# A convolution's running sum moved from SBUF to a PSUM bank, and small sums moved from that bank to another group

## The chip, the cores and the metric

One core of a Trainium2 chip runs the whole program in one launch. The metric is the device time of one execution in microseconds, the median of three runs. The engines are TensorE (PE, with PEld for its weight loads), VectorE (DVE), ScalarE (ACT), GpSimd (POOL) and SyncE (SP, which issues the DMAs).

## The reference

Two blocks on 512 tokens of width 1024, all in float32. The first is an attention block; the change doesn't touch it. The second has a mixer, a cross attention to 256 memory rows, and a feed-forward part. This is the mixer, cut to what matters:

```python
def hybrid_mixer(h, positions, ...):
    proj = h @ w_in
    q, k = partial_rope(proj's q), partial_rope(proj's k)      # 4 heads, 2 x 64 each
    a = diff_attention(q, k, v, lam)                           # softmax(..)[0] - lam * softmax(..)[1]
    a = rmsnorm(a, subln_g) * (1.0 - lam_init)
    c = u[..., :512] * jax.nn.sigmoid(u[..., 512:])            # gated unit
    c = causal_dwconv(c, cv_dw_w) + cv_dw_b                    # 31 taps, 512 channels
    c = jax.nn.silu(layernorm(c, cv_ln_g, cv_ln_b))
    return concatenate([a, c], axis=-1) @ w_out

def cross_attention(h, m, w_cq, w_ckv, w_co):
    q, kv = h @ w_cq, m @ w_ckv                                # kv: the memory projection
    ...
```

## The kernel before

Products of float32 are made of three products of split operands (`mm3` and its like: high by high, high by low, low by high, all at line 131 of the profile); a split is a cast on ScalarE (L149, L224) and a subtraction (L150 for weights on GpSimd or VectorE, L225 on VectorE).

The mixer works on 128 channels by 512 tokens at a time. Its steps are written in a string, in program order:

```python
u0 u1 u2 u3 q0 f0 q1 f1 v1 v0 f3 m b0 b1 b3 c w3 k7 f2 k0 k3 k4 k1 w2 w0 l k5 b2 k2 k6 w1
```

`u` is a quarter of the gated unit (L739 and L740 evacuate its two projections from a linear bank), `q` projects and rotates q and k of two heads (L795 to L800), `v` projects the values (L820), `f` is a head's front: scores, maxima (L843), softmax and difference (L847, L848), with L862 as its last instruction. `b` is a head's back (`diff_back`): transposes, product with the values, column sums of squares (L863 takes them), a root in small steps and a broadcast over partitions. `m` prepares the memory's rows and broadcasts their factors, `k` and `w` are pieces of the memory projection (256 columns; `k` is evacuated at L904), `c` is the convolution and `l` the layer norm over its four results (mean at L965 and L966, then L969, sums of squares, root, broadcast, and L983 to the splits).

The convolution has four quarters `cps[0..3]` of 128 channels. In each, tap 0 is L939, six taps are products on ScalarE (L944, L947) summed by GpSimd (L948) in a tile of their own, and the remaining taps, 92 in all, are one VectorE instruction each (L951): product with a weight per partition plus the running sum. L952 adds GpSimd's part.

PSUM has eight banks, in four groups: three linear ones (`lin`), three for scores (`z`), one `pv`, one small (`sm`). A tile takes the next bank of its group in program order, and waits until the tile that had it is read. Each engine's own order of instructions is made by a scheduler from the program order and these dependencies, with a cost estimate of its own, so that instructions of several steps stand mixed on an engine; on the chip each engine keeps its order.

Of the kernel before, what the change touches and what calls it, by code (L numbers as in the profile page):

```python
# [98 lines left out]
def block_kernel(ctx, tc, wts, vec, c_row, lam_v, cst, x_t, mem_t, mem_n, pos, out):  # L99
# [161 lines left out]
    msb = const.tile([P, P], BF16, name="msb")  # L261
    mfox = const.tile([P, P], BF16, name="mfox")

    def col_sums(accs):

        o = ps_sm()
        for a, acc in enumerate(accs):
            for i in range(NT):
                pe.matmul(o[:, a * NT + i:a * NT + i + 1], lhsT=acc[:, i * P:(i + 1) * P],
                          rhs=ones[:, 0:1], start=True, stop=True)  # L270
        return o[:, :len(accs) * NT]
# [40 lines left out]
            mm(o, ch[:, i:i + 1].to_broadcast([P, P]), identr, i == 0, False)  # L312
            mm(o, cl[:, i:i + 1].to_broadcast([P, P]), identr, False, i == nt - 1)

    def bcast(col, o, nt=NT, eng=dve):

        b = ps_sm()
        bcast_mm(col, b, nt, eng)
        act.copy(out=o, in_=b[:, :nt * P])

# [531 lines left out]
    def diff_back(h, pt, s0):  # L852
        tt = transposed(pt, b2p, {"z": ps_z, "lin": ps_lin, "pv": ps_pv}[TR_TAG])
        pv = ps_pv()
        for c in (3, 2, 1, 0):
            hc = slice(h * P, (h + 1) * P)
            mm3(pv[:, :(c + 1) * P], v2h[:, c, hc], v2l[:, c, hc], tt[c][0], tt[c][1], c == 3, c == 0)
        ah = b2p.tile([P, T], F32, tag="at", bufs=2, name="ah")
        aq = smp.tile([P, T], F32, tag="sq", name="aq")
        act.copy(out=ah, in_=pv)  # L860
        act.activation(out=aq, in_=pv, func=AF.Square)
        dve.scalar_tensor_tensor(out=s0, in0=s0, scalar=EPS, in1=s0, op0=ALU.mult, op1=ALU.mult)  # L862
        dve.scalar_tensor_tensor(out=s0, in0=col_sums([aq]), scalar=1.0 / P, in1=s0, op0=ALU.mult, op1=ALU.add)  # L863
        rsq_bits(s0, s0)
        ar = smp.tile([P, T], F32, tag="sq", name="ar")
        bcast(s0, ar)
        dve.tensor_tensor(out=ah, in0=ah, in1=ar, op=ALU.mult)
        return scaled_split(ah, sg8)

# [6 lines left out]
    def memory():  # L876
        mem_r = mem_t.rearrange("(k p) m -> p k m", p=P)
        msum = b2p.tile([P, 2], F32, name="msum")
        for i in range(2):
            raw = wrp.tile([P, D], F32, tag="wr", name="wr")  # L880
            nc.sync.dma_start(out=raw, in_=mem_n[i * P:(i + 1) * P])
            act.activation(out=raw, in_=raw, func=AF.Square, accum_out=msum[:, i:i + 1])
        rsq(mrc, msum, D)
        for j in range(2):
            raw = wrp.tile([P, D], F32, tag="wr", name="wr")
            nc.sync.dma_start(out=raw.rearrange("p (k m) -> p k m", k=4), in_=mem_r[:, 4 * j:4 * j + 4])
            for a in range(2):
                hi, lo = htile(), htile()
                src = raw[:, a * T:(a + 1) * T]
                for e in range(2):  # L890
                    k = 4 * j + 2 * a + e
                    m = slice(e * NM, (e + 1) * NM)
                    g = V("g_mem", k)
                    act.activation(out=hi[:, m], in_=src[:, m], func=AF.Identity, scale=g)
                    dve.scalar_tensor_tensor(out=lo[:, m], in0=src[:, m], scalar=g, in1=f32(hi[:, m]),
                                             op0=ALU.mult, op1=ALU.subtract)
                    ms.append((hi[:, m], lo[:, m]))
        bcast(mrc, mrb, 2)

    def mem_k(c):  # L900
        o = ps_lin()
# [28 lines left out]
    def conv():  # L930
        for c in range(4):
            cp = cps[c]

            def tap(j):
                return cp[:, 30 - j:30 - j + T], V("cv_w", c * 31 + j)

            ca = b2p.tile([P, PADW], F32, tag="cp", bufs=CP_BUFS, name="ca")[:, :T]
            x_, w_ = tap(0)
            dve.tensor_scalar(out=ca, in0=x_, scalar1=w_, scalar2=V("cv_b", c), op0=ALU.mult, op1=ALU.add)  # L939
            cb_ = (rb[:, 1], nacc[:, 0])[c % 2]  # L940
            for j in range(1, 1 + CONV_POOL):
                x_, w_ = tap(j)
                if j == 1:
                    act.activation(out=cb_, in_=x_, func=AF.Copy, scale=w_)  # L944
                else:
                    pr = b2p.tile([P, T], F32, tag="cpr", bufs=2, name="cpr")
                    act.activation(out=pr, in_=x_, func=AF.Copy, scale=w_)  # L947
                    pool.tensor_tensor(out=cb_, in0=cb_, in1=pr, op=ALU.add)  # L948
            for j in range(1 + CONV_POOL, 31):
                x_, w_ = tap(j)  # L950
                dve.scalar_tensor_tensor(out=ca, in0=x_, scalar=w_, in1=ca, op0=ALU.mult, op1=ALU.add)  # L951
            dve.tensor_tensor(out=ca, in0=ca, in1=cb_, op=ALU.add)  # L952
            cacc.append(ca)
            if c == 1:
                csum.append(nacc[:, 1])
                pool.tensor_tensor(out=csum[0], in0=cacc[0], in1=ca, op=ALU.add)
            elif c == 2:
                pool.tensor_tensor(out=csum[0], in0=csum[0], in1=ca, op=ALU.add)
# [356 lines left out]
```

## Time and profile before

| | us |
|---|---|
| median of three runs (1295.78 to 1298.67) | 1297.72 |
| the profiled execution | 1297.69 |
| its span | 1295.9 |
| TensorE busy | 1203.8 |
| VectorE busy | 849.7 |

The span is the time from the profile's first to its last instruction; 1.79 us of the profiled execution lie around it. The mean granted clock of TensorE was 0.968 of full speed. Busy times are summed over the span; the mixer's part around the convolution is about 507 to 753 us of it.

### The profile page before, as it was taken

The page shows a single profiled execution, that of the slowest core. Times are in us where ns is not written, and L with a number is a line of the kernel's source. Part 1 is how long each engine was busy: PE and PEld are TensorE (multiplying, and loading weights), DVE is VectorE, ACT ScalarE, POOL GpSimd, SP SyncE. Part 2 cuts the span into 40 slices and gives each one's busy share as a digit, 9 for nine tenths or more (in the row PEclk, how much of TensorE's full clock was granted, in tenths as well). Part 3 has the DMA queues.
Part 4 walks back from the last instruction along what each step waited for, and adds up shares of the span by engine and source line. Part 5 has one row for each costly group of instructions (what it writes and reads, how often), then busy time and mean ns, then how long its engine had stood idle before and what let it go on. Part 6 is the DMA issues. An engine that isn't in the chain of part 4 may idle for free.

```text
span 1295.9 us, 16574 instructions
## 1 busy us (share of the span) xinstructions
PE 1203.8 (93%) x6254; PEld 1022.9 (79%) x6254; DVE 849.7 (66%) x1250; ACT 594.5 (46%) x987; POOL 473.5 (37%) x299
## 2 busy tenths in 40 slices
PE   3899999999999999758699999999999999999996
PEld 2788879888878888657688887887888888888886
DVE  6867785655733757999998557456587777771112
ACT  4465655566333553324565635444444444442221
POOL 4534443222122384656543238104422222222222
PEclk9999999999989999879899799999999999999998
DMA  9242222222563332111243244311333332322321
GB/s 368 105 145 75 74 87 69 82 74 94 179 238 99 121 99 82 65 49 57 82 148 125 67 126 146 92 39 66 97 98 98 98 98 98 98 90 90 94 85 65
DMA packets 44960, 134.83 MB, mean 104 GB/s; under 512 B 4945, under 2 KB 10577, under 8 KB 44882
## 3 DMA queue, kind: packets, MB, share of 16 engines
q1 hardware_dynamic: 44882, 133.79, 32.3%
q8 instruction: 49, 0.80, 0.2%
q14 instruction: 29, 0.24, 0.1%
HBM read 124.33 MB, written 6.29 MB: 101 GB/s over the span
## 4 chain that ended last, share of the span: by engine, by line
PE 71%; DVE 20%; ACT 3%; issue 2%; DMA 2%; POOL 1%; SPq 0%; DVEq 0%; POOLq 0%; ACTq 0%
PE lin L131 61%; DVE ca L951 7%; PE z L131 5%; PE pv L131 2%; DMA wr<-in_wts 1%; PE z L457 1%; DVE h L232 1%; DVE ar L374 1%; ACT wh L149 1%; POOL wl L150 1%; DVE wl L150 1%; DVE smc L847 1%; DVE nm L843 1%; DVE h L225 1%; DVE xr L723 1%
## 5 line engine op out<-in xcount | busy, mean ns | idle before, releaser
L131 PE MATMUL lin<-h,wh 128*128 128x512 f32 (+1 forms) x2296 | 709.1, 389 | 11.1 <-ACT h L224 5.0
L131 PEld LDWEIGHTS lin<-h,wh 128*128 128x128 f32 x2296 | 426.2, 190 | 95.1 <-ACT h L224 5.4
L131 PE MATMUL lin<-h,wl 128*128 128x512 f32 (+1 forms) x1148 | 443.9, 387 | 2.7 <-POOL wl L150 1.8
L150 POOL TENSOR_TENSOR wl<-wr,wh 128x1024 fp32r<-128x1024 f32 (+1 forms) x110 | 272.5, 2478 | 461.8 <-ACT wh L149 442.8
L149 ACT CAST wh<-wr 128x1024 fp32r<-128x1024 f32 x189 | 196.7, 1043 | 255.2 <-PE lin L131 194.1
L131 PEld LDWEIGHTS lin<-h,wl 128*128 128x128 f32 x1148 | 217.6, 190 | 44.9 <-POOL wl L150 2.2
L150 DVE TENSOR_TENSOR wl<-wr,wh 128x1024 fp32r<-128x1024 f32 (+1 forms) x79 | 103.0, 1304 | 122.3 <-ACT wh L149 121.6
L131 PE MATMUL lin<-wh,h 128*128 128x256 f32 x656 | 136.5, 303 | 11.3 <-DVE cp L739 9.4
L131 PEld LDWEIGHTS lin<-wh,h 128*128 128x128 f32 x656 | 114.0, 209 | 12.5 <-DVE cp L739 9.6
L951 DVE SCALAR_TENSOR_TENSOR ca<-cp,vecs,ca 128x512 f32<-128x512 f32 x92 | 107.4, 1205 | 0.3
L1138 DVE SCALAR_TENSOR_TENSOR cv<-up,vecs,cv 128x512 f32<-128x512 f32 x88 | 94.5, 1074 | 17.9 <-ACT cv L1136 16.4
L131 PE MATMUL lin<-wl,h 128*128 128x256 f32 x328 | 99.0, 302 | 0.0
L131 PE MATMUL lin<-zz,wh 128*128 128x512 f32 (+1 forms) x324 | 92.4, 370 | 0.0
L131 PEld LDWEIGHTS lin<-wl,h 128*128 128x128 f32 x328 | 68.8, 210 | 0.2
L131 PEld LDWEIGHTS lin<-zz,wh 128*128 128x128 f32 x324 | 58.5, 188 | 11.4
L131 PE MATMUL lin<-zz,wl 128*128 128x512 f32 (+1 forms) x162 | 60.0, 370 | 0.0
L327 POOL TENSOR_TENSOR nacc<-nacc,sq 128x512 f32<-128x512 f32 x34 | 52.5, 1554 | 17.1 <-ACT sq L326 16.7
L1133 POOL MEMSET up<- 128x2 f32 x44 | 4.3, 100 | 148.5 <-DVE cv L1138 116.4
L528 POOL TENSOR_TENSOR zs<-zs,y 64x512 f32<-64x512 f32 x16 | 26.5, 1654 | 72.6 <-DVE y L527 70.3
L542 DVE TENSOR_TENSOR_SCAN om<-om 128x511 f32<-128x511 f32 (+3 forms) x32 | 36.7, 1186 | 8.2 <-ACT om L538 8.0
L1145 ACT ACTIVATE cv<-cv 128x512 f32<-128x512 f32 x22 | 13.9, 632 | 59.9 <-DVE cv L1138 59.9
L1134 DVE TENSOR_TENSOR up<-lin,rb 128x512 f32<-128x512 f32 x44 | 30.1, 687 | 16.3 <-PE lin L131 13.7
(364 smaller groups left out, 1662.6 us busy)
## 6 DMA issues: line engine op xcount, KB each, us to landing
wr<-in_wts SPq DMA_DIRECT2D x189, 512.0 KB, 3.6
ar<-in_wts SPq DMA_DIRECT2D x20, 512.0 KB, 10.2
qk<-qk SPq DMA_DIRECT2D x24, 128.0 KB, 2.2
wr<-in_wts SPq DMA_DIRECT2D x8, 384.0 KB, 3.0
xt<-in_x_t SPq DMA_DIRECT2D x4, 512.0 KB, 5.9
ma_d<-gt SPq DMA_DIRECT2D x8, 256.0 KB, 4.1
ma<-ma_d SPq DMA_DIRECT2D x8, 256.0 KB, 3.4
xr<-in_x_t SPq DMA_DIRECT2D x2, 1024.0 KB, 7.0
```

The source lines that it names most:

```text
L131: pe.matmul(o, lhsT=lhsT, rhs=rhs, start=start, stop=stop, skip_group_check=True)
L149: act.copy(out=hi[:, :n], in_=raw[:, :n])
L150: lo_engine().tensor_tensor(out=lo[:, :n], in0=raw[:, :n], in1=f32(hi[:, :n]), op=ALU.subtract)
L225: dve.tensor_tensor(out=lo, in0=src, in1=f32(hi), op=ALU.subtract)
L232: dve.scalar_tensor_tensor(out=lo, in0=src, scalar=g, in1=f32(hi), op0=ALU.mult, op1=ALU.subtract)
L327: pool.tensor_tensor(out=acc, in0=acc, in1=q, op=ALU.add)
L528: pool.tensor_tensor(out=zs[r], in0=zs[r], in1=y[r], op=ALU.mult)
L542: dve.tensor_tensor_scan(out=om[:, o:e], data0=om[:, o:e], data1=om[:, o:e], initial=1.0, op0=ALU.mult, op1=ALU.bypass)
L951: dve.scalar_tensor_tensor(out=ca, in0=x_, scalar=w_, in1=ca, op0=ALU.mult, op1=ALU.add)
L1134: dve.tensor_tensor(out=up[:, :T], in0=o, in1=rb[:, 0], op=ALU.mult)
L1138: dve.scalar_tensor_tensor(out=r, in0=up[:, 2 - j:2 - j + T], scalar=V("ffn_w", c * 3 + j), in1=r, op0=ALU.mult, op1=ALU.add)
L1145: act.activation(out=a, in_=a, func=AF.Silu)
```

## The change

The convolution's running sum `ca`, an SBUF tile, becomes `cz` in the one bank of `sm`. The four quarters so follow each other through one bank. Only the last instruction, which adds GpSimd's part, writes the SBUF tile `ca`, which is now allocated there. So that the bank is free for this, the column sums and the broadcast of a head's back, and the broadcast of the memory's factors, take a bank of `lin` in place of `sm`. Other users of `sm` stay. The number of instructions that work is the same.

```diff
-    def col_sums(accs):
-        o = ps_sm()
+    def col_sums(accs, ps_=None):
+        o = (ps_ or ps_sm)()
...
-    def bcast(col, o, nt=NT, eng=dve):
-        b = ps_sm()
+    def bcast(col, o, nt=NT, eng=dve, ps_=None):
+        b = (ps_ or ps_sm)()
...
-        dve.scalar_tensor_tensor(out=s0, in0=col_sums([aq]), scalar=1.0 / P, in1=s0, op0=ALU.mult, op1=ALU.add)
+        dve.scalar_tensor_tensor(out=s0, in0=col_sums([aq], ps_lin), scalar=1.0 / P, in1=s0, op0=ALU.mult, op1=ALU.add)
         rsq_bits(s0, s0)
         ar = smp.tile([P, T], F32, tag="sq", name="ar")
-        bcast(s0, ar)
+        bcast(s0, ar, ps_=ps_lin)
...
-        bcast(mrc, mrb, 2)
+        bcast(mrc, mrb, 2, ps_=ps_lin)
...
-            ca = b2p.tile([P, PADW], F32, tag="cp", bufs=CP_BUFS, name="ca")[:, :T]
+            cz = ps_sm()
             x_, w_ = tap(0)
-            dve.tensor_scalar(out=ca, in0=x_, scalar1=w_, scalar2=V("cv_b", c), op0=ALU.mult, op1=ALU.add)
+            dve.tensor_scalar(out=cz, in0=x_, scalar1=w_, scalar2=V("cv_b", c), op0=ALU.mult, op1=ALU.add)
...
             for j in range(1 + CONV_POOL, 31):
                 x_, w_ = tap(j)
-                dve.scalar_tensor_tensor(out=ca, in0=x_, scalar=w_, in1=ca, op0=ALU.mult, op1=ALU.add)
-            dve.tensor_tensor(out=ca, in0=ca, in1=cb_, op=ALU.add)
+                dve.scalar_tensor_tensor(out=cz, in0=x_, scalar=w_, in1=cz, op0=ALU.mult, op1=ALU.add)
+            ca = b2p.tile([P, PADW], F32, tag="cp", bufs=CP_BUFS, name="ca")[:, :T]
+            dve.tensor_tensor(out=ca, in0=cz, in1=cb_, op=ALU.add)
```

In the changed file the lines of the convolution are shifted: tap 0 is L940, the taps are L952, the last addition L954.

VectorE's order at the start of the convolution, before (the numbers behind the names are those of the tiles; `cp_4399` and `cp_4468` are the first two quarters' inputs, `ca_6052` and `ca_6097` their sums, `lin` the gated unit's projections):

```order
L951 SCALAR_TENSOR_TENSOR ca_6052<-cp_4399,vecs_78,ca_6052 128x512 x3
L939 TENSOR_SCALAR ca_6097<-cp_4468,vecs_78 128x512
L951 SCALAR_TENSOR_TENSOR ca_6052<-cp_4399,vecs_78,ca_6052 128x512
L739 TENSOR_TENSOR cp_4537<-lin_4539,rb_4291 128x512
L951 SCALAR_TENSOR_TENSOR ca_6097<-cp_4468,vecs_78,ca_6097 128x512
L951 SCALAR_TENSOR_TENSOR ca_6052<-cp_4399,vecs_78,ca_6052 128x512
L951 SCALAR_TENSOR_TENSOR ca_6097<-cp_4468,vecs_78,ca_6097 128x512
L951 SCALAR_TENSOR_TENSOR ca_6052<-cp_4399,vecs_78,ca_6052 128x512
```

And now, from the first addition to the first rotation (L795):

```order
L952 SCALAR_TENSOR_TENSOR sm_6052<-cp_4399,vecs_78,sm_6052 128x512 x4
L739 TENSOR_TENSOR cp_4537<-lin_4539,rb_4291 128x512
L952 SCALAR_TENSOR_TENSOR sm_6052<-cp_4399,vecs_78,sm_6052 128x512 x5
L740 TENSOR_TENSOR sg_4601<-lin_4570,rb_4291 128x512
L952 SCALAR_TENSOR_TENSOR sm_6052<-cp_4399,vecs_78,sm_6052 128x512 x6
L739 TENSOR_TENSOR cp_4606<-lin_4608,rb_4291 128x512
L952 SCALAR_TENSOR_TENSOR sm_6052<-cp_4399,vecs_78,sm_6052 128x512 x6
L740 TENSOR_TENSOR sg_4670<-lin_4639,rb_4291 128x512
L952 SCALAR_TENSOR_TENSOR sm_6052<-cp_4399,vecs_78,sm_6052 128x512 x2
L795 TENSOR_TENSOR ro_4788<-h_4785,cosb_4366 128x64
```

Two quarters went side by side there, and 40 additions stood ahead of the first rotation (4, 7, 7, 7 and 15 between the evacuations); now one quarter goes alone, and 23 stand there. The second quarter begins after the first one's last addition, which takes GpSimd's part `rb_4291`, behind two rotations:

```order
L799 TENSOR_TENSOR h_4798<-ro_4801,ro_4802 128x8x8
L800 TENSOR_TENSOR h_4798<-ro_4803,ro_4804 128x8x8
L954 TENSOR_TENSOR ca_6096<-sm_6052,rb_4291 128x512
L940 TENSOR_SCALAR sm_6098<-cp_4468,vecs_78 128x512
L952 SCALAR_TENSOR_TENSOR sm_6098<-cp_4468,vecs_78,sm_6098 128x512 x3
L795 TENSOR_TENSOR ro_4924<-h_4921,cosb_4366 128x64
```

The last quarter's last addition stood ahead of the first L904; now it stands behind the backs of heads 0 and 1 and within the front of head 2, and all eight L904 stand behind that front.

TensorE's order at the start of the memory projection, before (`lin_5532` is the last product of the values, `lin_6234` the first of the memory projection, step w3):

```order
L131 MATMUL lin_5532<-wh_5589,h_4277 128x256
L131 MATMUL lin_5532<-wl_5590,h_4277 128x256
L131 MATMUL lin_5532<-wh_5589,h_4278 128x256
...
L131 MATMUL lin_6234<-wh_6237,h_5764 128x256
L131 MATMUL lin_6234<-wl_6238,h_5764 128x256
L131 MATMUL lin_6234<-wh_6237,h_5765 128x256
```

And now (the same step is `lin_6238`; `lin_6033` is the broadcast of head 3's back, `lin_6011` its column sums, `pv_6813` and `pv_6822` transposes of head 2's back):

```order
L131 MATMUL z_6420<-kl0o_4394,qk_6340 128x256
L131 LDWEIGHTS identb_90
L131 MATMUL z_6420<-mfox_94,identb_90 128x128
L269 MATMUL lin_6011<-ones_86,aq_6007 128x1 x4
L457 MATMUL pv_6813<-idf_79,p_6363 128x128
...
L457 MATMUL pv_6822<-idf_79,p_6363 128x128
L131 MATMUL lin_6033<-identr_91,bch_6034 128x128
L131 MATMUL lin_6238<-wh_6241,h_5764 128x256
L131 MATMUL lin_6238<-wl_6242,h_5764 128x256
```

The 384 matmuls of the memory projection began four transposes after the last product of the values and stood among the fronts of heads 3 and 2 and the backs of heads 0, 1 and 3. Now they begin behind all of these: 264 of them, the norm's mean and sums, 24, the sums and the broadcast of head 2's back, and the last 96.

## Rows read from the trace of the kernel before

**Rows 1.** The page's first part: busy time, share of the span, instructions.

```profile
PE 1203.8 (93%) x6254; PEld 1022.9 (79%) x6254; DVE 849.7 (66%) x1250; ACT 594.5 (46%) x987; POOL 473.5 (37%) x299
```

**Rows 2.** The chain that ended last: start, duration, engine, tile, line, count.

```profile
538.54 24.65 DVE ca L951 x15
```

**Rows 3.** Stretches of the mixer: busy time of each engine, granted clock, DMA.

```profile
core 0: us, PE busy (x) PEld busy (x) DVE busy (x) ACT busy (x) POOL busy (x), PEclk, DMA share, GB/s
507.00:545.00 38.00, 28.63 (x159) 25.63 (x158) 37.93 (x37) 10.73 (x14) 21.67 (x10) 0.87 0.20 67
545.00:602.00 57.00, 38.84 (x278) 37.11 (x277) 56.62 (x71) 22.41 (x36) 35.19 (x20) 0.85 0.17 51
602.00:665.00 63.00, 49.38 (x337) 46.49 (x338) 62.32 (x107) 36.53 (x79) 33.08 (x18) 0.86 0.31 96
665.00:723.00 58.00, 52.08 (x390) 47.91 (x388) 52.25 (x117) 36.36 (x82) 25.58 (x12) 0.96 0.44 135
723.00:753.00 30.00, 28.60 (x188) 27.65 (x188) 17.98 (x43) 16.38 (x25) 9.15 (x4) 0.79 0.19 54
```

**Rows 4.** The tile ca: count, ns min/median/max, first and last start.

```profile
L951 DVE SCALAR_TENSOR_TENSOR ca<-cp,vecs,ca x92: 727/742/2893, 507.7 to 670.2; 128x512 f32<-128x512 f32 x92
```

**Rows 5.** Timeline of VectorE, 530 to 575: start, duration, instruction.

```profile
533.23 4.71 DVE L951 SCALAR_TENSOR_TENSOR ca<-cp,vecs,ca 128x512 f32<-128x512 f32 x7
...
570.44 2.97 DVE L951 SCALAR_TENSOR_TENSOR ca<-cp,vecs,ca 128x512 f32<-128x512 f32 x4
```

**Rows 6.** Timeline of GpSimd at 539, with the idle time before.

```profile
539.29 1.74 POOL L742 TENSOR_TENSOR cp<-cp,sg 128x512 f32<-128x512 f32 x1 [7.79 <-ACT sg L741]
```

**Rows 7.** Groups of GpSimd, 507 to 672: busy us, mean ns, idle before.

```profile
L150 POOL TENSOR_TENSOR wl<-wr,wh 128x1024 fp32r<-128x1024 f32 x18 | 47.7, 2652 | 27.7 <-ACT wh L149 27.7
L948 POOL TENSOR_TENSOR rb<-rb,cpr 128x512 f32<-128x512 f32 x12 | 18.8, 1571 | 2.8 <-ACT cpr L947 2.6
```

**Rows 8.** Groups of VectorE over the whole span.

```profile
L1134 DVE TENSOR_TENSOR up<-lin,rb 128x512 f32<-128x512 f32 x44 | 30.1, 687 | 16.3 <-PE lin L131 13.7 <-ACT rb L319 2.6
...
L798 DVE TENSOR_TENSOR ro<-h,sinb 128x64 f32<-128x64 f32 x8 | 6.1, 763 | 0.0
...
L904 DVE TENSOR_TENSOR kvo<-lin,mrb 128x256 f32<-128x256 f32 x8 | 3.3, 417 | 0.1
```

**Rows 9.** Timeline of VectorE from 717 on.

```profile
717.81 2.46 DVE L969 SCALAR_TENSOR_TENSOR ca<-lin,ca 128x512 f32<-128x512 f32 x4
...
722.07 0.22 DVE L847 SCALAR_TENSOR_TENSOR smc<-s,nlam,smc 128x1 f32<-128x1 f32 x1 [0.29 <-ACT p L845]
...
722.79 0.15 DVE L862 SCALAR_TENSOR_TENSOR s<-s 128x4 f32<-128x4 f32 x1
...
727.05 0.16 DVE L309 TENSOR_TENSOR bcl<-s,bch 128x4 fp32r<-128x4 f32 x1 [0.26 <-ACT bch L308]
...
736.26 2.48 DVE L983 TENSOR_TENSOR ca<-ca,lin 128x512 f32<-128x512 f32 x4 [2.71 <-PE lin L131]
...
748.50 0.68 DVE L225 TENSOR_TENSOR h<-ca,h 128x512 fp32r<-128x512 f32 x1
```

**Rows 10.** VectorE's line L847 alone in the fronts after 665.

```profile
665.00:723.00 58.00, 8.69 (x11) 0.96 0.44 135
```

**Rows 11.** Timeline of TensorE at the end of the gated unit.

```profile
523.12 0.28 PE L131 MATMUL lin<-wh,h 128*128 128x256 f32 x1
...
533.36 0.58 PE L131 MATMUL lin<-wh,h 128*128 128x256 f32 x1 [9.37 <-DVE cp L739]
```

**Rows 12.** Timeline of TensorE from the last product of the values to the stage's end.

```profile
664.49 0.28 PE L131 MATMUL lin<-wh,h 128*128 128x256 f32 x1
664.61 0.40 PE L131 MATMUL lin<-h,wh 128*128 128x256 f32 x2
...
715.10 1.02 PE L965 MATMUL lin<-nacc,ones 128*128 128x512 f32 x2
...
730.78 0.47 PE L131 MATMUL lin<-identr,bch 128*128 128x128 f32 x1
...
751.91 0.28 PE L131 MATMUL lin<-wh,h 128*128 128x256 f32 x1
```

## The prediction

> **What bounds the kernel now.** I read the page's head first: TensorE is busy for 93% of the span [rows 1]. So a change on VectorE counts only where TensorE waits for it. Next comes the chain that ended last. In the mixer of the second block it runs through the convolution's VectorE instruction; its longest piece is 24.65 us for fifteen of them [rows 2]. The table by stage shows the stage of the change, 507 to 753 us: up to 665 VectorE is busy for 37.93 of 38, 56.62 of 57 and 62.32 of 63 us, and TensorE for 28.63, 38.84 and 49.38 [rows 3]. From 723 it turns round: TensorE 28.60 of 30, VectorE 17.98. So the first 160 us are VectorE's, the last 30 TensorE's, and what lies between is both. Outside the stage nothing changes, so the whole answer is where the mixer's last 256-column matmul stands (751.91 us before).
>
> The convolution's 92 tap additions (L951) take 107.41 us, 727 to 2893 ns each with a median of 742 [rows 4]. The timeline says why they spread: seven follow each other in 4.71 us from 533.23 [rows 5], where GpSimd stands idle for 7.79 us up to 539.29 [rows 6], and the next fifteen are the 24.65 us of the chain, when it works again. In 507 to 672 its part is eighteen weight subtractions (L150) and two times twelve tap sums (L948) [rows 7]. VectorE instructions of the same size that read one operand from PSUM don't spread: forty-four average 687 ns [rows 8].
>
> **What each part of the change does.**
>
> *Taps in PSUM.* Each of the 92 then has one SBUF operand and the running sum in PSUM. Its price: no row shows VectorE writing PSUM at this size. From below, four PSUM-reading ones follow each other in 2.46 us [rows 9], about 0.61 each. From above, the contended mean of today, 107.41/92 = 1.17. Of one chain back to back in SBUF the trace has four in 2.97 us, the first on another tile: (2.97 − 0.73 − 0.66)/2 = 0.79, against (4.71 − 0.74)/6 = 0.66 for the alternating tiles of before [rows 5]. The new order has one chain at a time (one bank), first in runs of four to six and later one by one between other instructions. I take 0.70, nearest to the SBUF chain's rows: 92 × 0.70 = 64 us. Today's 107.4 overlap by some 0.08 each, so they cover 100. The saving is 36 us of VectorE.
>
> The Trainium skill's page "SBUF — State Buffer", section "Who interferes with whom", says that a VectorE instruction with two SBUF inputs contends with a GpSimd instruction that reads SBUF, and one with at most one does not; the trace agrees (727 to 2893 ns against 687). The Trainium skill's page "Perfetto Trace Analysis", section "Optimizing Scalar/DVE Operations", speaks against the change: about 125 ns of access overhead for VectorE on PSUM, about 60 on SBUF. By that the 92 would cost 92 × 0.065 = 6 us more and the end be 1306 (an estimate from that page); the PSUM-reading rows here show no such penalty for reading.
>
> *VectorE up to the end of the fronts.* From 507 to 723 it is busy for 37.93 + 56.62 + 62.32 + 52.25 = 209.1 us and idle for 6.9 [rows 3]. Less the 36. Less the norm's four (2.46) and five evacuations of the memory projection (L904, 0.417 each [rows 8]), which move behind: 4.5. Less contention in the fronts after 665: there the eleven instructions of L847 take 8.69 us [rows 10], where an undisturbed one takes 0.22 [rows 9], so 6.3 are excess, and by the same look at L848, L288 and L309 I put as much again; GpSimd does there the memory weights' subtractions, which now wait for banks (next part). I take 13 off, with 0 and 20 as bounds. Busy: 209.1 − 36 − 4.5 − 13 = 155.6.
>
> Idle comes in at the front. Between the evacuations of the gated unit and the first rotation VectorE's order has 4, 5, 6, 6 and 2 additions, where it had 4, 7, 7, 7 and 15. TensorE's stall of 9.37 us behind L739 [rows 11] mostly goes. But VectorE reaches the rotation at 507 + 23 × 0.79 + 4 × 0.6 = 528, and the first projection, begun at 523.12 [rows 11], needs 96 × 0.12 = 11.5 us plus the copy to SBUF: 7 us of wait. Then L954 of the first channel, which now must come before the second channel can begin (L940 takes the one bank again), waits for GpSimd's six sums: an estimate from their 1.57 us and the subtractions between [rows 7] puts these at 542, 4.5 us more. Behind it stand the other rotations, so TensorE's scores wait too. With the 6.9 of before: 18.5 idle. The last front then ends at 507 + 155.6 + 18.5 = 681, where before has 722.79 [rows 9]: 42 us gained there. TensorE allows it: the six projections of q, k and v are 576 matmuls, 69 us from 523, with scores and transposes about 605.
>
> *Small sums in the linear banks.* This gives the gain back. The three linear banks go round in program order. The sums and broadcasts of the heads' back parts (b0, b1, b3) stand in it before the memory projection, so TensorE's order no longer begins with that when the v projection ends (as at 664.49 to 664.61 [rows 12]) and works on it under f3 and f2. It begins it behind b3's broadcast, which waits for VectorE: the front's end plus the root's small steps (722.79 to 727.05 before, 4.3 us [rows 9]): 681 + 4 = 685. From there everything is serial:
> - 264 matmuls at 0.12 [rows 12]: 31.7 us.
> - The norm: before, from 715.10 (mean) to 730.78 (broadcast) 15.7 us [rows 12], with other work between on every engine. I take 11, part of b2's products within: of the 15.7 the fronts' and b2's instructions fill about a third.
> - 24 matmuls and the rest of the broadcast: 3.
> - From L983 to the last split before: 736.26 to 749.18, 12.9 us [rows 9]. b2's broadcast now stands behind that split on VectorE and ahead of 96 matmuls on TensorE; six matmuls and eight column sums are all its cover. Bounds 8 and 13; I take 10.5.
> - 96 matmuls, the broadcast and the rest of b2's products: 13.4.
> - After two waits TensorE's granted clock falls to half, as in 723 to 753 (0.79 [rows 3]): 1.5.
>
> Sum 71 us; the stage ends at 685 + 71 = 756. b2's broadcast, which came after 752 in before and held TensorE there for 1.7, is then done: 754.3 against 751.9 [rows 12]. The change costs 2.4 us. Against the profiled execution, 1297.69 (the span and 1.79 around it), that is 1300.1; the median shown, 1297.72, is the same to 0.03. I say **1300**.
>
> **Rivals.**
>
> *The gain reaches the end.* If VectorE's other instructions before 665 lose their stretching too (their neighbours on GpSimd run faster without L951), or the waits at the front are hidden, b3's broadcast comes at about 670: 670 + 71 − 1.7 = 739, 1285. For it: the rotation's step L798 averages 763 ns for 64 columns [rows 8], more than 512 columns from PSUM. Against: GpSimd has the same work in less time. Below 680 for that broadcast the change is a gain of over 0.2%.
>
> *A longer tail.* If the single bank leaves VectorE idle for another 10 us (it waits for six GpSimd sums at each channel's end, with nothing of the convolution to fill in), b3's broadcast is at 695, and if the norm's waits are as long as before (15.7 and 12.9) the tail is 78: 695 + 78 − 1.7 = 771, 1317. It decides from b3's broadcast after 685 with a tail of 71 (the sum above stands at that edge), or from a tail over 71 behind 685. For it: the order has nothing beside those waits on TensorE. Against: less GpSimd contention there.
>
> *Adding in one PSUM bank is slow.* If write and next read of the same bank cost 0.95 us, the 92 take 23 us more: 1323. For it: nothing here shows such a chain, and the SBUF chain already goes from 0.66 to 0.79. Against: PSUM reads at 0.61. The overhead that the Trainium skill's page "Perfetto Trace Analysis" states, in the section named above, would be a quarter of this.
>
> *The change doesn't do what it says:* the taps stay as stretched as before, with one SBUF operand too. Then 36 us of VectorE come back while the serial tail stays: 1336. Against it stand the forty-four at 687 ns, though GpSimd is less busy beside those.
>
> **How the numbers follow.** The trade 0.50, the gain at the end 0.27, the longer tail 0.15, slow PSUM 0.05, no relief 0.03. About 0.2% (2.6 us) is what a measurement of this kernel can tell from no change. The likeliest case's own range is 1292 to 1309 (8 us either way on 685, from the 13 off and the front's idle, and 4 on 71). Of it 0.08 lie below 1295, 0.17 within, 0.25 above 1300.3. Faster: 0.08 + 0.27 = 0.35; same: 0.17 and 0.02 from the edge of the longer tail: 0.19; slower 0.46. The range takes in the gain down to 1278 and the longer tail to 1319.
>
> **What the profile after would show.** Right: the taps 0.65 to 0.80 us each, with a narrow spread; TensorE without the 9 us stall at 524 but with the memory projection beginning late, at 677 to 693, behind a broadcast into a linear bank; gaps of TensorE of some 10 us in the norm and again before b2's broadcast; the first 512-column matmuls of the output product near 754. Wrong: taps over 0.9 us, or memory matmuls under the fronts of heads 3 and 2, or b3's broadcast before 675 or after 695.

## The result and the profile after

The changed kernel takes **1304.17 us** (median; 1300.48 to 1306.35) where the kernel before, on the same chips, takes 1296.89. The ratio is 1.0058, with a 95% interval of 1.0044 to 1.0072: the change costs 7.3 us, between 5.7 and 9.3. The forecast of 1300.0 had the sign and the mechanism, and a price of 2.4 us that is too low by about five. The profiled execution took 1302.44 us, its span is 1300.5, and the mean granted clock 0.963.

The page's first part of after, against [rows 1]:

```profile
PE 1209.3 (93%) x6254; PEld 1025.0 (79%) x6254; DVE 802.7 (62%) x1250; ACT 596.3 (46%) x987; POOL 460.2 (35%) x299
```

VectorE's busy time falls by 47 us and the kernel gets slower: less time of this engine is not by itself less time of the kernel. The five stretches of [rows 3], after the change:

```profile
core 0: us, PE busy (x) PEld busy (x) DVE busy (x) ACT busy (x) POOL busy (x), PEclk, DMA share, GB/s
507.00:545.00 38.00, 38.00 (x260) 35.39 (x258) 28.48 (x44) 17.40 (x26) 30.05 (x18) 1.00 0.30 91
545.00:602.00 57.00, 46.95 (x358) 44.18 (x357) 55.94 (x96) 37.99 (x73) 36.72 (x24) 0.93 0.29 91
602.00:665.00 63.00, 44.34 (x234) 36.54 (x233) 62.35 (x145) 29.31 (x72) 9.15 (x5) 0.74 0.16 51
665.00:723.00 58.00, 48.45 (x337) 45.46 (x335) 21.26 (x60) 25.58 (x48) 27.54 (x12) 0.85 0.42 119
723.00:753.00 30.00, 18.95 (x121) 18.70 (x121) 12.63 (x33) 13.44 (x20) 6.01 (x3) 0.72 0.11 39
```

Read the matmul counts. In the first two rows TensorE issues 618 where it issued 437: the stall behind the gated unit is gone. From 602 to 665 it issues 234 instead of 337, at a granted clock of 0.74: it has run out of work and waits on the chains of the fronts and backs. What released it last was ScalarE's softmax (L844) in 7.5 us of these waits, VectorE in 5.7 and a transfer of `qk` in 3.2, and VectorE, which feeds these chains, is as full as before. In the last row, 723 to 753, it is busy for 18.95 of 30 us where it was busy for 28.60. What was won in front is lost behind. The tap additions themselves, in the view of the tile `sm`, against [rows 4]:

```profile
L952 DVE SCALAR_TENSOR_TENSOR sm<-cp,vecs,sm x92: 731/754/757, 506.9 to 667.8; 128x512 f32<-128x512 f32 x92
...
L940 DVE TENSOR_SCALAR sm<-cp,vecs x4: 803/806/814, 505.6 to 637.4; 128x512 f32<-128x512 f32 x4
L954 DVE TENSOR_TENSOR ca<-sm,rb x2: 691/692/692, 540.8 to 635.6; 128x512 f32<-128x512 f32 x2
```

The spread of 727 to 2893 ns has become 731 to 757. VectorE's timeline at the front, and where the fronts end (against [rows 5] and [rows 9]):

```profile
514.93 4.70 DVE L952 SCALAR_TENSOR_TENSOR sm<-cp,vecs,sm 128x512 f32<-128x512 f32 x6
...
525.36 1.54 DVE L952 SCALAR_TENSOR_TENSOR sm<-cp,vecs,sm 128x512 f32<-128x512 f32 x2
533.93 0.52 DVE L795 TENSOR_TENSOR ro<-h,cosb 128x64 f32<-128x64 f32 x1 [7.04 <-ACT h L788]
...
540.78 0.69 DVE L954 TENSOR_TENSOR ca<-sm,rb 128x512 f32<-128x512 f32 x1 [1.32 <-POOL rb L949]
...
675.86 0.15 DVE L862 SCALAR_TENSOR_TENSOR s<-s 128x4 f32<-128x4 f32 x1
...
680.47 0.15 DVE L309 TENSOR_TENSOR bcl<-s,bch 128x4 fp32r<-128x4 f32 x1
```

The first L952 row is one chain back to back: (4.70 − 0.76)/5 = 0.79 us each. The last front ends at 675.86 where it ended at 722.79. And TensorE from there, against [rows 12]:

```profile
679.97 0.47 PE L131 MATMUL lin<-identr,bch 128*128 128x128 f32 x1 [0.77 <-ACT bch L308]
680.24 0.52 PE L131 MATMUL lin<-wh,h 128*128 128x256 f32 x1
...
716.64 1.02 PE L967 MATMUL lin<-nacc,ones 128*128 128x512 f32 x2
...
722.70 1.36 PE L131 MATMUL lin<-ones,cpr 128*128 128x1 f32 x8 [3.55 <-POOL cpr L977]
...
726.18 1.86 PE L131 MATMUL lin<-ones,cpr 128*128 128x1 f32 x8 [2.12 <-POOL cpr L977]
729.77 0.48 PE L131 MATMUL lin<-identr,bch 128*128 128x128 f32 x1 [1.73 <-ACT bch L308]
...
735.28 0.95 PE L269 MATMUL lin<-ones,aq 128*128 128x1 f32 x8
...
743.43 0.48 PE L131 MATMUL lin<-identr,bch 128*128 128x128 f32 x1 [7.20 <-ACT bch L308]
...
757.57 0.63 PE L131 MATMUL lin<-h,wh 128*128 128x512 f32 x2
```

680.24 is the first matmul of the memory projection, right behind the first one of the broadcast of head 3's back, as forecast: before it stood at 664.61, under the fronts. The four bracketed waits from 722.70 on have nothing beside them. The stage ends at 757.5, 5.5 us later than before.

**How stages are compared below.** The first tap (L939, L940) starts between 501.4 and 507.1 us in the profiled executions of the fourteen kernels, though no edit is made to what lies ahead of it. So a stage's length is taken here from the start of its own first tap to the start of the last addition of the output product (into `xr`), in one profile of each kernel: 295.3 us before, 300.9 after. "Broadcast" is that of head 3's back (VectorE's L309 in it), from the first tap: 220.4 us before, 174.9 after. Ratios are of medians, to the kernel before on the same chip (1294.96 to 1295.34 us).

### The profile page after: what moved, and what is told of

It is laid out like the page before. It is cut to its first block, busy times and chain, and to the rows that moved or that the text cites. A ratio compares the mean times of both kernels' runs of the same rounds, so it can differ in the third digit from the quotient of the medians.

```text
span 1300.5 us, 16580 instructions
## 1 busy us (share of the span) xinstructions
PE 1209.3 (93%) x6254; PEld 1025.0 (79%) x6254; DVE 802.7 (62%) x1250; ACT 596.3 (46%) x987; POOL 460.2 (35%) x299
## 5 line engine op out<-in xcount | busy, mean ns | idle before, releaser
L150 POOL TENSOR_TENSOR wl<-wr,wh 128x1024 fp32r<-128x1024 f32 (+1 forms) x110 | 268.0, 2438 | 486.6 <-ACT wh L149 467.6
L150 DVE TENSOR_TENSOR wl<-wr,wh 128x1024 fp32r<-128x1024 f32 (+1 forms) x79 | 103.0, 1304 | 125.3 <-ACT wh L149 124.6
L131 PE MATMUL lin<-wh,h 128*128 128x256 f32 x656 | 126.2, 290 | 2.5 <-DVE v2l L820 2.5
L131 PEld LDWEIGHTS lin<-wh,h 128*128 128x128 f32 x656 | 106.5, 197 | 2.9 <-DVE v2l L820 2.8
L131 PE MATMUL lin<-wl,h 128*128 128x256 f32 x328 | 95.4, 291 | 0.0
L952 DVE SCALAR_TENSOR_TENSOR sm<-cp,vecs,sm 128x512 f32<-128x512 f32 x92 | 69.0, 750 | 1.3
L131 PEld LDWEIGHTS lin<-wl,h 128*128 128x128 f32 x328 | 64.8, 197 | 0.1
L131 PE MATMUL z<-qk 128*128 128x512 f32 (+3 forms) x96 | 37.8, 398 | 11.7 <-ACT p L844 6.4
L542 DVE TENSOR_TENSOR_SCAN om<-om 128x511 f32<-128x511 f32 (+3 forms) x32 | 36.7, 1187 | 8.2 <-ACT om L538 8.0
```

The costliest lines, as they stand in the source:

```text
L131: pe.matmul(o, lhsT=lhsT, rhs=rhs, start=start, stop=stop, skip_group_check=True)
L150: lo_engine().tensor_tensor(out=lo[:, :n], in0=raw[:, :n], in1=f32(hi[:, :n]), op=ALU.subtract)
L542: dve.tensor_tensor_scan(out=om[:, o:e], data0=om[:, o:e], data1=om[:, o:e], initial=1.0, op0=ALU.mult, op1=ALU.bypass)
L952: dve.scalar_tensor_tensor(out=cz, in0=x_, scalar=w_, in1=cz, op0=ALU.mult, op1=ALU.add)
```

## Experiments

The prediction's theory, called A, is the trade: taps in PSUM save about 36 us of VectorE, and the small sums in the linear banks make TensorE's memory projection wait for a broadcast, so that the saving is lost behind it.

### 1. The banks alone

```diff
-            cz = ps_sm()
+            ca = b2p.tile([P, PADW], F32, tag="cp", bufs=CP_BUFS, name="ca")[:, :T]
...
-                dve.scalar_tensor_tensor(out=cz, in0=x_, scalar=w_, in1=cz, op0=ALU.mult, op1=ALU.add)
+                dve.scalar_tensor_tensor(out=ca, in0=x_, scalar=w_, in1=ca, op0=ALU.mult, op1=ALU.add)
```

> Only the small sums move to the linear banks; the taps stay in an SBUF tile. Theory A (the linear banks' order puts the memory projection behind head 3's broadcast, and only the faster taps pay for that): the projection begins behind that broadcast at about 715 to 725 us, since the taps are as stretched as before, and a serial tail of some 78 us follows as in the changed kernel: the stage ends 35 to 50 us later than before, 1330 to 1347. Theory B (the single bank and the single chain of the convolution are what cost the gain, the sums' new place is neutral): 1292 to 1302, as before.

Measured: 1325.87 us, 1.0248 [1.0229, 1.0267]. Half of the change alone costs 31 us by the medians, and the other half gives some 24 back, since the whole costs 7. TensorE, at the broadcast and at the stage's end:

```profile
703.73 0.47 PE L131 MATMUL lin<-identr,bch 128*128 128x128 f32 x1
704.00 0.52 PE L131 MATMUL lin<-wh,h 128*128 128x256 f32 x1
...
782.11 0.63 PE L131 MATMUL lin<-h,wh 128*128 128x512 f32 x2
```

From broadcast to end 78.4 us, in after 77.6: the tail is the same whatever the taps cost. It starts 22.7 us later, counted from the first tap, because VectorE is late: over its stretch from the first tap to the last front it is busy for 188.85 of 194.15 us, in after for 157.53 of 170.45. So the 31.3 us of busy time that the PSUM taps save arrive as 23.7, the rest is VectorE's waits at the front (idle 5.3 to 12.9). The time lies below A's 1330 to 1347 and far above B's 1292 to 1302. A's size was too large because the fronts end at 700.62: taking the memory projection from under them relieves VectorE more than A had it. VectorE's groups up to the last front show where (line, busy us, mean ns, idle before); before:

```profile
L951 DVE SCALAR_TENSOR_TENSOR ca<-cp,vecs,ca 128x512 f32<-128x512 f32 x92 | 107.4, 1205 | 0.3
...
L847 DVE SCALAR_TENSOR_TENSOR smc<-s,nlam,smc 128x1 f32<-128x1 f32 x16 | 10.8, 672 | 2.2 <-ACT p L845 2.0
```

and with the banks alone:

```profile
L951 DVE SCALAR_TENSOR_TENSOR ca<-cp,vecs,ca 128x512 f32<-128x512 f32 x92 | 107.2, 1203 | 0.3
...
L847 DVE SCALAR_TENSOR_TENSOR smc<-s,nlam,smc 128x1 f32<-128x1 f32 x16 | 4.4, 274 | 0.7 <-ACT p L845 0.6
```

The taps keep their price to 0.2 us; L847 falls by 6.4.

### 2. The small sums in the bank `pv`

```diff
-        dve.scalar_tensor_tensor(out=s0, in0=col_sums([aq], ps_lin), ...)
+        dve.scalar_tensor_tensor(out=s0, in0=col_sums([aq], ps_pv), ...)
...
-        bcast(s0, ar, ps_=ps_lin)
+        bcast(s0, ar, ps_=ps_pv)
```

(and the same for the memory's factors)

> The taps in PSUM as in the change, the small sums in the bank of the products with the values (pv) in place of the linear ones. Theory A: the memory projection begins when the values are done (about 607 us) and runs under the fronts, the 264 matmuls (32 us) leave the tail, head 3's broadcast stays at 680 to 690: 1268 to 1282. Theory B: the taps' single bank keeps holding everything up: 1300 to 1306, as the change.

Measured: 1288.63 us, 0.9953 [0.9934, 0.9972], between A's 1268 to 1282 and B's 1300 to 1306; the stage is 287.5 us long, 13.4 less than after. With the linear banks free of broadcasts the memory projection starts under the fronts again. Two stretches:

```profile
600.00:665.00 65.00, 56.21 (x422) 53.48 (x421) 63.19 (x111) 30.41 (x60) 32.27 (x14) 0.93 0.46 141
665.00:720.00 55.00, 37.12 (x148) 30.66 (x149) 32.59 (x96) 24.77 (x58) 4.89 (x3) 0.55 0.07 24
```

422 matmuls up to 665 against 234 of after in nearly the same time. But `pv` is one bank, which the backs' products need too: behind 665 TensorE is busy for 37 of 55 us, at a granted clock of 0.55, and 19.4 us of its waits stand before instructions that write `pv`. Head 3's broadcast, which A had at 680 to 690, comes at 715.9. The wait has moved from one bank group to another. That the bank group decides A's loss is shown here, and that `pv` has a wait of its own.

### 3. Part of the memory projection ahead of the backs

The bank groups stay as the change has them; two orders of steps put 168 and 72 of the memory projection's matmuls ahead of the backs.

```diff
-MIX = "... f3 m b0 b1 b3 c w3 k7 f2 k0 k3 k4 k1 w2 w0 l k5 b2 k2 k6 w1"
+MIX = "... f3 m w3 k7 k0 k3 k4 k1 b0 b1 b3 c f2 w2 w0 l k5 b2 k2 k6 w1"
```

> The change, with six pieces of the memory projection (w3 k7 k0 k3 k4 k1, 168 matmuls) placed ahead of the backs of heads 0, 1 and 3 in the program order; banks as in the change. Theory A: 168 x 0.12 = 20 us leave the tail and hide under the fronts: 1281 to 1291. Theory B: no change, 1300 to 1306.

```diff
+MIX = "... f3 m w3 k7 b0 b1 b3 c f2 k0 k3 k4 k1 w2 w0 l k5 b2 k2 k6 w1"
```

> The same with two pieces only (w3 k7, 72 matmuls). Theory A: 72 x 0.12 = 8.6 us leave the tail: 1292 to 1299. Theory B: 1300 to 1306.

Measured: with 168 ahead 1291.98 us, 0.9978 [0.9959, 0.9997], a microsecond above A's range; with 72 ahead 1301.87, 1.0063 [1.0044, 1.0082], in B's. Against after the stages are 10.9 and 0.2 us shorter, where 168 and 72 matmuls at 0.12 are 20 and 8.6. What is missing stands in the broadcast, 12.2 and 7.6 us later than in after. Matmuls moved under the fronts are no gift: the fronts end later with them. What comes with them are evacuations, weight subtractions and a share of TensorE's order; only the subtractions are tested alone, in experiment 4. Two rows of VectorE with 168 ahead:

```profile
634.00 2.31 DVE L862 SCALAR_TENSOR_TENSOR s<-s 128x4 f32<-128x4 f32 x1
636.24 0.41 DVE L904 TENSOR_TENSOR kvo<-lin,mrb 128x256 f32<-128x256 f32 x1
```

L862, four elements a row, takes 2.31 us there, beside the last of three weight subtractions that end on GpSimd at 636.29, and 0.15 or 0.16 in each of the four fronts of after. An evacuation L904 that stood behind the fronts now stands within them.

### 4. The memory weights without their low part

To see how much of those 12.2 us GpSimd's subtractions (L150) make, these two kernels leave them out for the memory weights: the products with the low part take the high part again, so all matmuls stay. One has the order with 168 ahead, the other, as control, the order of the change.

```diff
-    def unit(name, j, n=D):
+    def unit(name, j, n=D, lo=True):
...
+        if not lo:
...
+            return hi, hi
...
-        lin_k(o[:, :NM], unit("mk", c), 0, ms)
+        lin_k(o[:, :NM], unit("mk", c, lo=False), 0, ms)
...
```

(and the same for the weights of the memory's values)

> As the kernel with 168 matmuls of the memory projection ahead of the backs, but the memory projection's weights have no low part: GpSimd's subtractions (L150) for these twelve weights are left out and the high part stands in for the low one, with the same matmuls. Theory C (moving the projection back under the fronts gave only half of its 20 us, since GpSimd's subtractions then stretch VectorE's instructions in the fronts and head 3's broadcast comes 12 us later): that broadcast falls from 692.6 to 681 to 685, time 1280 to 1285. Theory D (the fronts are slowed by what else the projection brings, its evacuations and its share of TensorE and ScalarE): as without this edit, 1289 to 1295.

> Control: the change itself with the same subtractions left out. They stand in the tail there, where VectorE waits anyway, so by both theories nothing moves: 1299 to 1306.

Measured: 1286.87 us, 0.9934 [0.9916, 0.9953], between C's range and D's, and the control 1297.87, 1.0019 [1.0003, 1.0035], a microsecond below what both theories said. The broadcast stands at 187.1 us from the first tap with 168 ahead, at 179.2 without the subtractions; in after at 174.9, in the control at 171.8. So the price of 168 matmuls under the fronts is 12.2 us with the subtractions and 7.4 without: by these single profiles they make 4.8 of it, under half. L862 is back at 0.16 us. The control moved by 3 us as well, so the subtractions cost something wherever they stand. What makes the other 7.4 (evacuations, TensorE's time itself) was not taken apart.

### 5. The norm and head 2's back in the score banks

The tail's waits come from the norm and from head 2's broadcast, which hold the linear banks in program order. Here they get banks of `z`, whose scores are done by then.

```diff
-        lmean = ps_lin()
+        lmean = ps_z()
...
-        lvar = ps_lin()
+        lvar = ps_z()
...
-        lr = ps_lin()
+        lr = ps_z()
...
+        ps_ = ps_z if h == 2 else ps_lin
```

(`ps_` is then the group of head 2's sums and broadcast.)

> The change, with the layer norm's three tiles and head 2's sums and broadcast in banks of the scores (z), so that they don't stand in the linear banks' order. Theory A2 (the tail's two waits, 13.1 us from the norm's mean to its broadcast and 8.2 before head 2's broadcast, are bare only because the next memory pieces need the banks of these tiles): the 384 matmuls run through both, the stage ends at 735 to 740: 1281 to 1288. Rival (the chain from the norm's mean over its splits to head 2's is itself as long as the tail): 1296 to 1304.

Measured: 1283.99 us, 0.9905 [0.9869, 0.9941], as A2 had it; the stage is 287.4 us, 13.5 less than after. Its stretch from 690 to 730, the norm's mean and the step on VectorE before its broadcast, and head 2's broadcast:

```profile
690.00:730.00 40.00, 40.00 (x334) 39.87 (x333) 11.95 (x22) 23.70 (x34) 28.17 (x12) 1.00 0.60 185
```

```profile
672.42 2.02 PE L968 MATMUL z<-nacc,ones 128*128 128x512 f32 x2
...
702.99 0.17 DVE L309 TENSOR_TENSOR bcl<-muc,bch 128x4 fp32r<-128x4 f32 x1 [0.26 <-ACT bch L308]
...
734.74 1.09 PE L131 MATMUL lin<-h,wh 128*128 128x512 f32 x4
...
740.55 0.33 PE L131 MATMUL z<-identr,bch 128*128 128x128 f32 x1 [1.50 <-ACT bch L308]
```

TensorE is busy for 40.00 of 40 us through the second half of the norm and its broadcast, at full clock, and the output product's 512-column matmuls begin at 734.74, in after at 757.57; head 2's broadcast stands among them, where after waits 7.20 us for it. The norm itself is not faster: from its mean to its broadcast it takes 30.6 us (672.42 to 702.99), in after 13.1. Head 3's broadcast, with the norm's mean now ahead of it, comes 7.0 us later than in after (181.9 us from the first tap). Neither matters, since the norm has lost its hold on the banks and the memory projection runs beside it. So the waits of the tail are a matter of bank groups too, and the trade need not be one.

### 6. Both, and how many taps GpSimd takes

The order with 168 ahead on experiment 5's banks, with `l b2` ahead of the pieces that are left; and on that the number of a quarter's taps that go to ScalarE and GpSimd, nine and five where it was seven (seven products on ScalarE, not six, which GpSimd sums in six additions).

```diff
+MIX = "... f3 m w3 k7 k0 k3 k4 k1 b0 b1 b3 c f2 l b2 w2 w0 k5 k2 k6 w1"
```

> Both cures: 168 matmuls ahead of the backs, the norm and head 2's sums in z banks, and the norm and head 2's back ahead of the last 216 matmuls. By A2, with head 3's broadcast at 692 and 216 matmuls, products and broadcasts behind (26 + 9 us): stage end 727 to 733, 1272 to 1280. By the rival: 1286 to 1293.

```diff
-CONV_POOL = 7
+CONV_POOL = 9
```

> The best so far (z banks and 168 matmuls first, 1281.8) with eight taps of each quarter instead of six summed by GpSimd: VectorE loses 8 x 0.70 = 5.6 us, GpSimd gets 8 x 1.5 = 12. If VectorE's own time sets head 3's broadcast: 5 us earlier, 1276 to 1279. If VectorE waits for GpSimd's sums at a quarter's end (1.32 us today) or is stretched by them elsewhere: 1281 to 1288.

```diff
-CONV_POOL = 7
+CONV_POOL = 5
```

> The other way: four taps of each quarter on GpSimd, VectorE gets 5.6 us more, GpSimd 12 less. If VectorE's own time sets the broadcast: 1285 to 1289. If GpSimd's sums cost VectorE's other instructions more than they save (1.3 us for each that is stretched): 1275 to 1281.

Measured: with seven 1281.78 us, 0.9884 [0.9853, 0.9916]; with nine 1278.91, 0.9878 [0.9839, 0.9916]; with five **1273.56**, 0.9837 [0.9799, 0.9876]. The stages are 280.5, 281.3 and 273.4 us. The kernel with seven misses both of its ranges (1272 to 1280 and 1286 to 1293): head 3's broadcast comes at 695.3 where 692 was taken, and the last 256-column matmul at 736.5 where 727 to 733 was expected. Nine taps off take eight additions from VectorE and win nothing that can be told. Their median lies in the range that was given for a gain from VectorE's own time, but head 3's broadcast is not 5 us earlier: it comes 193.2 us from the first tap, with seven 190.1. Five taps off give VectorE eight additions more and win 7.1 us of the stage, some 6 by the ratios of the medians; that is the side of contention, 1.4 us below the range given for it. With nine, VectorE's timeline has two long waits for projected heads that ScalarE has not yet copied:

```profile
535.50 0.51 DVE L795 TENSOR_TENSOR ro<-h,cosb 128x64 f32<-128x64 f32 x1 [8.51 <-ACT h L788]
...
547.02 0.35 DVE L795 TENSOR_TENSOR ro<-h,cosb 128x64 f32<-128x64 f32 x1 [6.01 <-ACT h L788]
```

With seven they are 7.04 and 0.78. With five, the first wait is 5.46, the second is gone, and the last addition of the first quarter, which with seven waits 1.32 for GpSimd, does so no more:

```profile
529.77 0.51 DVE L795 TENSOR_TENSOR ro<-h,cosb 128x64 f32<-128x64 f32 x1 [5.46 <-ACT h L788]
...
531.59 0.69 DVE L955 TENSOR_TENSOR ca<-sm,rb 128x512 f32<-128x512 f32 x1
```

More than the waits, other instructions got cheaper. VectorE's groups from the first tap to the convolution's last addition, with seven taps off:

```profile
L953 DVE SCALAR_TENSOR_TENSOR sm<-cp,vecs,sm 128x512 f32<-128x512 f32 x92 | 69.1, 751 | 1.3
...
L799 DVE TENSOR_TENSOR h<-ro 128x64 f32<-128x64 f32 x8 | 8.0, 996 | 0.1
...
L798 DVE TENSOR_TENSOR ro<-h,sinb 128x64 f32<-128x64 f32 x8 | 5.0, 630 | 0.0
```

and with five:

```profile
L953 DVE SCALAR_TENSOR_TENSOR sm<-cp,vecs,sm 128x512 f32<-128x512 f32 x100 | 75.0, 750 | 1.7
...
L799 DVE TENSOR_TENSOR h<-ro 128x64 f32<-128x64 f32 x8 | 4.9, 610 | 0.0
...
L798 DVE TENSOR_TENSOR ro<-h,sinb 128x64 f32<-128x64 f32 x8 | 1.7, 213 | 0.0
```

The eight additions cost 5.9 us more. The rotations, whose operands lie in SBUF, cost less: their six lines, L795 to L800, fall from 31.3 us in sum to 18.7. Over the whole stretch VectorE is busy for 148.58 us with seven and 143.34 with five, so all but the taps went from 79.5 to 68.3. The Trainium skill's page "Perfetto Trace Analysis", section "Optimizing Scalar/DVE Operations", warns that offloading between VectorE and GpSimd might not help, because they share an SBUF read port; these two kernels agree, by 7.1 us of the stage.

### 7. Where the memory projection stands

Two more orders on the same banks, seven taps off: the 168 matmuls among the backs, and 240 of the 384 ahead of them.

```diff
+MIX = "... f3 m w3 b0 k7 k0 b1 k3 k4 b3 c k1 f2 l b2 w2 w0 k5 k2 k6 w1"
```

> As the best so far, but the 168 matmuls' pieces stand between the backs of heads 0, 1 and 3 in place of ahead of them. If what counts is only that they come before head 3's broadcast: 1279 to 1284. If their banks then wait for each back's broadcast: later by up to 5 us, 1283 to 1288.

```diff
+MIX = "... f3 m w3 k7 k0 k3 k4 k1 k5 k2 k6 b0 b1 b3 c f2 l b2 w2 w0 w1"
```

> As the best so far with all nine 256-column key pieces ahead (w3 and all k, 240 matmuls in place of 168). By the full price 72 x 0.12 = 8.6 us leave the tail: 1273 to 1276. By what the earlier runs showed (of 8.6 us moved under the fronts 0.2 came back, of 20 us 11) the fronts give most of it back: 1278 to 1283.

Measured: 1281.8 us, 0.9894 [0.986, 0.9928], and 1274.7, 0.9838 [0.9804, 0.9872]. Both are as the first theory of each had them. Spreading the matmuls changes nothing by the medians against the first order of experiment 6; 72 more of them ahead shorten the stage by 7.1 us, of the 8.6 that they take, though head 3's broadcast comes 8.7 us later (198.8 us from the first tap). In experiment 3, with the norm and head 2's sums in the linear banks, 72 ahead won only 0.2. The five taps and this order together were not run.

## Why the prediction was right, and where its sizes were off

**The trade** is shown by its halves: the banks alone cost 31 us, the taps then give some 24 back. **The taps:** 0.70 was taken for each, with the row of the SBUF chain at 0.79 as the nearest; back to back they run at 0.79, with small instructions between them at 0.66 (from 643.34 to 644.00 in VectorE's timeline), so 0.70 was a fair mean. Their busy sum is 69.0 where it was 107.4. What was not foreseen is that the contention moved: the rotations became dearer. Two of their lines, from the first tap to the last front, before:

```profile
L799 DVE TENSOR_TENSOR h<-ro 128x64 f32<-128x64 f32 x8 | 2.9, 363 | 0.0
...
L800 DVE TENSOR_TENSOR h<-ro 128x64 f32<-128x64 f32 x8 | 1.7, 211 | 0.0
```

and after:

```profile
L799 DVE TENSOR_TENSOR h<-ro 128x64 f32<-128x64 f32 x8 | 8.0, 996 | 0.1
L800 DVE TENSOR_TENSOR h<-ro 128x64 f32<-128x64 f32 x8 | 7.2, 905 | 0.0
```

That is 10.6 us given back, 9.7 over all six lines of the rotation (21.3 to 31.0): instructions with two SBUF operands beside GpSimd's sums and weight subtractions (L150), which now meet them instead of the taps. In after each of the eighteen rotation instructions over 0.4 us overlaps an instruction of GpSimd, the longest a subtraction, and none of the 22 that overlap none is that long. The Trainium skill's page "SBUF — State Buffer", section "Who interferes with whom", has the rule for both (two SBUF inputs contend with GpSimd's reads, at most one does not), and the trace agrees: the taps with one SBUF operand stay at 731 to 757 ns, L800 with two goes from 211 to 905. The working's sum had applied it to the taps alone.

**The end of the fronts** was forecast at 681 and came at 676. Busy 155.6 forecast, 157.5 measured; idle 18.5 forecast, 12.9 measured (the wait for the rotation 7 forecast and 7.04 measured, the one for GpSimd's sums 4.5 and 1.32); and the stage began 1.4 us earlier. The relief of the fronts, 13 with bounds 0 and 20, is by experiment 1 some 17.6: its fronts end 22.2 us sooner than before, less the 4.5 of L904 and the norm that moved. So the sum came near, in part by luck: the rotations' loss, which the working did not have, is covered by a larger relief and shorter waits.

**The tail** is the step that failed in size: 71 us forecast from the broadcast, 77.6 measured. From the rows of TensorE: 36.7 up to the norm's mean (716.64 − 679.97; forecast 31.7, which counted the 264 matmuls, but not the rest of the broadcast and the part of head 2's products that comes there), 13.1 for the norm (11), 5.5 for the 24 matmuls (3), 8.2 up to head 2's broadcast (10.5) and 14.1 behind it (13.4). The norm and the wait together are as forecast, 21.3 against 21.5. The largest part of what was missing is the clock, taken at 1.5 us. TensorE from the broadcast on (its busy time and matmuls, the granted clock, DMA):

```profile
680.00:686.00 6.00, 6.00 (x29) 0.52 0.01 3
686.00:716.60 30.60, 30.60 (x253) 1.00 0.62 179
```

The granted clock is at about half there, 0.52, behind a stretch from 665 to 680 in which TensorE was busy for 9.00 of 15 us. The matmuls start 0.21 us apart where they do so every 0.12 us at full clock: 23 of them here, and 14 each behind the norm's broadcast and behind head 2's. That is 51 × 0.09 = 4.6 us, in three places where the forecast had two waits. The fronts' five microseconds cover most of the 6.6 in absolute time, so the stage ended at 757.5 where 756 was forecast: two errors of opposite sign.

**A gain that was taken too large:** 1.7 us were taken off because head 2's broadcast came after 752 before. Measured, the last 256-column matmul comes 5.5 us later than before and the last addition into `xr` 4.6, so 0.9 came back. Counted from the first tap, the first matmul of the broadcast was forecast at 178.4 and came at 174.4; 2.4 − 4.0 + 6.6 + 0.8 = 5.8 is near the longer stage. By the medians the loss is 7.3; the profiles show a stage longer by 5.6, and a start 1.1 us earlier that no edit explains. What is left, 1.7, lies within what single profiles differ by (the stage's starts alone by 5.7).

**The rivals.** The gain at the end needed the broadcast below 680 with a tail of 71; it came at 680 with 77.6. The longer tail came true in its length, 77.6 against 78, but by luck: its norm and its wait were to be 15.7 and 12.9 and are 13.1 and 8.2, and its late broadcast did not come. What lengthened the tail, the clock above all, it did not name. Slow adding in one bank is refuted by 754 ns against 742: 92 × 0.012 = 1.1 us. The 6 us estimated from the Trainium skill's page "Perfetto Trace Analysis", section "Optimizing Scalar/DVE Operations" (about 125 against 60 ns of access), don't show either, so the measurement decides. That the taps stay stretched is refuted by their spread.

## What to carry to other kernels

A PSUM bank group that is allotted in program order is a part of TensorE's order: before a small sum gets a bank from the group that the big products use, look at which products come behind it and what it waits for, and give it banks whose owners are done (here 31 us lost and 13.5 won by that alone). Freeing an engine pays only as far as what stands behind it can start earlier, so look at the order of the next engine first. And work shared out to an engine that contends with the one it relieves has to be counted with what it costs the other's instructions: here fewer taps on GpSimd, not more, gave the fastest kernel, 1.6% under the one before.

## What the runs showed of the hardware

- A running sum in PSUM costs VectorE hardly more than one in SBUF: 754 against 742 ns at the median, and 0.79 us for each link of an undisturbed chain in either place (in SBUF an estimate from [rows 5]).
- The first tap, a TENSOR_SCALAR from SBUF, is another matter: 806 ns into PSUM (L940 above), against 535 into SBUF. Its line in the tile `ca` before (ns min/median/max):

```profile
L939 DVE TENSOR_SCALAR ca<-cp,vecs x4: 532/535/1509, 506.6 to 589.1; 128x512 f32<-128x512 f32 x4
```

- GpSimd's sums are cheaper too beside the taps in PSUM: its tap sums in `rb` fell from 1571 ns [rows 7] to 1292, here in its groups from 507 to 680 of after:

```profile
L949 POOL TENSOR_TENSOR rb<-rb,cpr 128x512 f32<-128x512 f32 x12 | 15.5, 1292 | 9.3 <-ACT cpr L948 9.0
```

- The contention is not in proportion to size: 64-column rotations at 996 ns on average (L799), and four elements a row (L862) at 2.31 us, where undisturbed ones take 0.22 and 0.15.
